# Linear attention on one core: two of pair 3's output stores issued from SyncE in place of GpSimd

## The chip, the core and the metric

The kernel runs on one NeuronCore of a Trainium2 chip. The core has a matrix engine (TensorE, here PE), three engines for elementwise work (VectorE or DVE, ScalarE or ACT, GpSimd or POOL), a SyncE (SP) that here only issues transfers, and 16 DMA engines that move data between the core's memory (SBUF) and HBM. PE writes its results to PSUM, from where DVE or ACT must take them.

A transfer is issued by an engine's instruction and then runs by itself. Those issued by POOL go over a software queue (q0 in the profile, "software_dynamic"), those issued by SP over a hardware queue (q1, "hardware_dynamic"). Both are worked off by the same 16 DMA engines.

The metric is the device time of one execution in microseconds (us), shorter is better. The time before is 125.52 us, the median of three runs (125.43 to 125.59).

## What is computed

Linear attention with the feature map relu(x) + 1, for 8 x 12 heads of 512 rows and 64 columns, float32 in and out:

```python
Q_feat = np.maximum(0, Q) + 1
K_feat = np.maximum(0, K) + 1
KV = np.einsum('bhkd,bhkv->bhdv', K_feat, V)
K_sum = np.sum(K_feat, axis=2)
numerator = np.einsum('bhqd,bhdv->bhqv', Q_feat, KV)
denominator = np.einsum('bhqd,bhd->bhq', Q_feat, K_sum)
return numerator / (denominator[:, :, :, None] + 1e-10)
```

The three inputs are 12.58 MB each and so is the output: 37.75 MB are read from HBM and 12.58 MB written.

## The kernel before

The 96 heads are cut into six equal parts of 16 heads, called pairs and numbered 0 to 5 (each is a pair of halves `n` for keys and values). For one pair, each of Q, K and V is 2 MiB of float32 in HBM; POOL's loads turn it into bfloat16 on the way, so that 1 MiB is written to SBUF. One output pair is 2 MiB of float32 and leaves in two stores of 1 MiB; only the last pair leaves in three (1 MiB, 0.5 MiB, 0.5 MiB), as `stores_of` (line 311) says.

For each pair: `k_features` (line 155, DVE) makes the key features `kf`; `v_block` (168, DVE or ACT) spreads V into a block form `v_all` with a column of ones, which gives the denominators; `keys_values` (183, PE) multiplies the two into PSUM in four parts for each half; `weights` (196, ACT) copies the result to SBUF; `q_features` (172, DVE), `transposes` (205, PE) and `transposed` (212, ACT) bring the query features into the form that PE needs; `out_matmuls` (217, PE) makes one of eight output parts in PSUM; `norms` (231, DVE) takes a reciprocal of the denominators (line 236), multiplies (line 237) and so writes that part into the pair's output tile `o_sb`; `store` (147) sends parts of it to HBM.

The order on each engine is written out by hand in `ORDER` (line 23). A word is a letter for the task, a pair, and indices: `n41` is the norm of pair 4, part 1; `s30` and `s31` are the two stores of pair 3, parts 0 to 3 and parts 4 to 7; `lk5` is the load of pair 5's keys. Each engine works through its own list in order; where a task needs the result of another engine it waits on a semaphore, and everything behind it on that engine waits too. `needs` (270) lists what a task must come after.

What matters around the change:

- POOL's list has all loads first and then ten stores, in the order `s01 s00 s30 s11 s10 s20 s21 s31 s40 s41`. A store waits on POOL until DVE has written its parts: s30 for n30 to n33 (of which n32 comes last in DVE's list), s31 for n34 to n37 (n36 comes last).
- SP's list has `s50 s51 s52`, the last pair's stores. SP also issues the very first load (`load_first_k`, line 124).
- `store` gets the engine that issues it as an argument (line 341), and asks for a single packet only on POOL's queue (line 152). In HBM a row piece of one store is 2 KB long (8 rows of 64 float32).
- The output tiles come from a pool of four buffers (`OUT_BUFS`, line 15). The first key load borrows one, pairs 0 to 3 have one each, and pair 4 takes over that of pair 0, pair 5 that of pair 1. So the first norm of pair 4 (n41) must come after the stores s00 and s01 have landed, and the first norm of pair 5 (n50) after s10 and s11.
- PSUM has two buffers for output parts (`psum`), so PE's `out_matmuls` of a part waits until DVE's norm two parts earlier is through.
- DVE's list around pair 4's begin is `n35 n34 n37 v502 n36 f50 v501 n41 v513 v510 n40 v511 n43 f51 n42 n45 n44 n46 n47 n50 ...`: the key features (f51) and value blocks of pair 5 stand behind n41.

Of the kernel before, what the change touches and what calls it, by code (L numbers as in the profile page):

```python
# [41 lines left out]
        e31 v412 c41 v411 c42 c43 e40 v500 c50 v503 e41 c51 v512 c52 c53 e50 e51  # L42
    """,
    POOL="""
        lv2 lk2 lq2 lv3 lq3 lk3 lv4 lq4 lk4 lq5 lv5 lk5 s01 s00 s30 s11 s10 s20 s21 s31 s40 s41
    """,
    SP="""
        s50 s51 s52
    """,
)  # L50

# [2 lines left out]
def kernel(  # L54
# [12 lines left out]
    nc = tc.nc  # L67
# [66 lines left out]
    def load(x, s, ns=(0, 1)):  # L134
        if x == "q":
            load_q(s)
            return
        if (x, s) not in tiles:
            tiles[x, s] = pools[x].tile([P, 2, ROWS, D], BF16, name=f"{x}_raw")
        t = tiles[x, s]  # L140
        nc.gpsimd.dma_start(  # L141
            out=t[:, ns[0] : ns[-1] + 1], in_=drams[x][:, 2 * s + ns[0] : 2 * s + ns[-1] + 1]
        )
        for n in ns:
            raw[x, s, n] = t[:, n]

    def store(s, parts, engine):
        lo, hi = parts[0], parts[-1] + 1
        engine.dma_start(  # L149
            out=o_dram[:, 8 * s + lo : 8 * s + hi],  # L150
            in_=outs[s][:, lo:hi],
            single_packet=engine is nc.gpsimd,
        )

    def k_features(s, n):
        kf = kf_pool.tile([P, ROWS, 2, D], BF16, name="kf")
        for a in range(2):
            nc.vector.tensor_scalar(  # L158
                out=kf[:, :, a],
                in0=raw["k", s, n],  # L160
                scalar1=shift[:, a : a + 1],
                scalar2=least[:, a : a + 1],
                op0=ALU.add,
                op1=ALU.max,
            )
        kfs[s, n] = kf

    def v_block(s, n, b, copy):
        ps = slice(32 * b, 32 * b + 32)
        copy(out=v_alls[n][ps, :, b * D1 : b * D1 + D], in_=raw["v", s, n][ps])  # L170

    def q_features(s):
        qf = qf_pool.tile([P, R, C, D], BF16, name="qf")
        rows = raw["q", s].rearrange("p (r c) d -> p r c d", r=R)
        for i in range(C // 2):
            cs = slice(2 * i, 2 * i + 2)
            nc.vector.tensor_scalar(  # L177
                out=qf[:, :, cs], in0=rows[:, :, cs],
                scalar1=1.0, scalar2=1.0, op0=ALU.add, op1=ALU.max,
            )  # L180
        qfs[s] = qf

    def keys_values(s, n, part):

        if part == 0:
            kva_pss[s, n] = psum_kva.tile([P, 4 * D1], FP32, name="kva_ps")
        for c in range(part * ROWS // 4, part * ROWS // 4 + ROWS // 4):
            nc.tensor.matmul(  # L188
                kva_pss[s, n],
                lhsT=kfs[s, n][:, c].rearrange("p a d -> p (a d)"),  # L190
                rhs=v_alls[n][:, c],
                start=(c == 0),
                stop=(c == ROWS - 1),
            )

    def weights(s, n):
        kva_ps = kva_pss.pop((s, n))
        for x in range(2):
            for a in range(2):
                nc.scalar.copy(  # L200
                    out=kvas[s % 2][64 * x : 64 * x + 64, 8 * n + a : 8 * n + 8 : 2, x],
                    in_=kva_ps[64 * a : 64 * a + 64].rearrange("p (b d) -> p b d", b=4),
                )

    def transposes(s, i):
        qt_ps = qt_pss[s, i] = psum_qt.tile([P, R, P], BF16, name="qt_ps")
        for r in range(R):
            nc.tensor.transpose(  # L208
                qt_ps[:, r], qfs[s][:, r, 2 * i : 2 * i + 2].rearrange("p x d -> p (x d)"), identity
            )  # L210

    def transposed(s, i, copy):
        if s not in qts:
            qts[s] = mid_pool.tile([P, C // 2, P, R], BF16, name="qt")
        copy(out=qts[s][:, i], in_=qt_pss.pop((s, i)).rearrange("p r q -> p q r"))  # L215

    def out_matmuls(s, part):

        o_ps = o_pss[s, part] = psum.tile([P, 2, BANK], FP32, name="o_ps")
        for c in range(C // 2):  # L220
            for t in range(2):
                h = 2 * part + t
                nc.tensor.matmul(  # L223
                    o_ps[64 * t : 64 * t + 64, c // 2, (c % 2) * W : (c % 2) * W + W],
                    lhsT=qts[s][:, c, 8 * h : 8 * h + 8],
                    rhs=kvas[s % 2][:, h],
                    start=True,
                    stop=True,
                )

    def norms(s, part):
        if s not in outs:
            outs[s] = out_pool.tile([P, 8, C, D], FP32, name="o_sb")
        cells = o_pss.pop((s, part))[:, :, 0 : 2 * W].rearrange("p b (r x) -> p b r x", x=D1)
        recip = recip_pool.tile([P, 2, 4, 1], FP32, name="recip")
        nc.vector.reciprocal(out=recip, in_=cells[:, :, :, D:D1])  # L236
        nc.vector.tensor_tensor(  # L237
            out=outs[s][:, part].rearrange("p (b r) d -> p b r d", b=2),
            in0=cells[:, :, :, 0:D],
            in1=recip.to_broadcast([P, 2, 4, D]),  # L240
            op=ALU.mult,
        )
# [24 lines left out]
    last = NPAIR - 1  # L267
# [43 lines left out]
    def stores_of(s):  # L311

        if s < 0:
            return ()
        return (range(4), range(4, 8)) if s < last else (range(4), range(4, 6), range(6, 8))

    def trace(engine, task):
        x, s, *at = task
        if x == "load":
            load(at[0], s)  # L320
        elif x == "kf":
            k_features(s, at[0])
        elif x == "vb":
            copy = nc.vector.tensor_copy if engine == "DVE" else nc.scalar.copy
            v_block(s, at[0], at[1], copy)
        elif x == "qf":
            q_features(s)
        elif x == "kv":
            keys_values(s, *at)
        elif x == "ev":  # L330
            weights(s, at[0])
        elif x == "tr":
            transposes(s, at[0])
        elif x == "tc":
            transposed(s, at[0], nc.vector.tensor_copy if engine == "DVE" else nc.scalar.copy)
        elif x == "om":
            out_matmuls(s, at[0])
        elif x == "no":
            norms(s, at[0])
        elif x == "st":  # L340
            store(s, stores_of(s)[at[0]], nc.sync if s == last else nc.gpsimd)

    def read(word):
        if word[0] == "l":
# [3 lines left out]
    def trace_all(orders):  # L348

        left = {engine: list(tasks) for engine, tasks in orders.items()}  # L350
        while any(left.values()):
            before = len(done)
            for engine, tasks in left.items():
                while tasks and all(t in done or t[1] < 0 for t in needs(engine, tasks[0])):
                    trace(engine, tasks[0])
                    done.add(tasks.pop(0))
            assert len(done) > before, {e: t[:1] for e, t in left.items()}
# [54 lines left out]
```

## Time and profile before

| | |
|---|---|
| median of three runs | 125.52 us |
| the profiled execution | 125.7 us, span 123.9 us |
| PE busy (share of span) | 79.9 us (64%) |
| DVE | 94.9 us (77%) |
| ACT | 87.1 us (70%) |
| POOL | 25.6 us (21%) |
| HBM read and written | 37.75 and 12.58 MB, 406 GB/s over the span |
| software queue q0 | 6736 packets, 28.84 MB |
| hardware queue q1 | 1216 packets, 3.15 MB |
| granted PE clock, mean | 0.942 |

The span reaches from the first to the last instruction in the trace; the execution's own time has some 1.8 us more around it. Busy times are those in which an engine ran an instruction; waiting and issuing a transfer do not count for PE, DVE, ACT and SP. The bytes of the queues are those written, so a load that turns float32 into bfloat16 counts with half of what it reads from HBM. "Landing" is the moment at which a transfer's semaphore tells that all its data has arrived.

The ten stores on POOL's queue take 0.75 us each to issue, the three on SP's queue 0.37 us each.

### The profile page before, as it was taken

The page shows a single profiled execution, that of the slowest core. Times are in us where ns is not written, and L with a number is a line of the kernel's source. Part 1 is how long each engine was busy: PE and PEld are TensorE (multiplying, and loading weights), DVE is VectorE, ACT ScalarE, POOL GpSimd, SP SyncE. Part 2 cuts the span into 40 slices and gives each one's busy share as a digit, 9 for nine tenths or more (in the row PEclk, how much of TensorE's full clock was granted, in tenths as well). Part 3 has the DMA queues.
Part 4 walks back from the last instruction along what each step waited for, and adds up shares of the span by engine and source line. Part 5 has one row for each costly group of instructions (what it writes and reads, how often), then busy time and mean ns, then how long its engine had stood idle before and what let it go on. Part 6 is the DMA issues. An engine that isn't in the chain of part 4 may idle for free.

```text
span 123.9 us, 2350 instructions
## 1 busy us (share of the span) xinstructions
PE 79.9 (64%) x960; PEld 61.1 (49%) x960; DVE 94.9 (77%) x185; ACT 87.1 (70%) x97; POOL 25.6 (21%) x52
## 2 busy tenths in 40 slices
PE   0000059995696879972599999499897885975000
PEld 0000037883584656851467788268666563753000
DVE  4998996408996996973986996999999299899400
ACT  7548740599999996999509999899999995031000
POOL 6993002400004300060100019000662000220000
PEclk9999999999999999999559999999999999999755
DMA  3999999999999999999999999999999999999992
GB/s 95 333 214 220 220 201 221 213 227 214 200 216 212 227 213 210 222 220 200 212 221 227 205 212 221 213 214 212 216 328 422 414 419 413 417 411 417 408 399 98
DMA packets 7963, 32.13 MB, mean 259 GB/s; under 512 B 528, under 2 KB 528, under 8 KB 7056
## 3 DMA queue, kind: packets, MB, share of 16 engines
q0 software_dynamic: 6736, 28.84, 93.6%
q1 hardware_dynamic: 1216, 3.15, 6.7%
q8 instruction: 7, 0.11, 0.3%
q14 instruction: 4, 0.03, 0.1%
HBM read 37.75 MB, written 12.58 MB: 406 GB/s over the span
## 4 chain that ended last, share of the span: by engine, by line
DMA 32%; DVE 28%; issue 18%; PE 12%; POOL 2%; ACT 2%; DVEq 0%; POOLq 0%
DMA out_dram<-o_sb 18%; DMA q_raw<-in_Q_dram 15%; PE kva_ps L188 9%; DVE o_sb L237 8%; DVE v_all L170 5%; DVE v_all L262 4%; DVE v_all L260 4%; DVE kf L158 3%; DVE recip L236 2%; ACT qt L215 2%; PE o_ps L223 2%; POOL v_raw L141 1%; DVE qf L177 1%; PE qt_ps L208 1%; POOL out_dram L149 1%
## 5 line engine op out<-in xcount | busy, mean ns | idle before, releaser
L188 PE MATMUL kva_ps<-v_all,kf 128*128 128x260 bf16 x384 | 51.9, 287 | 21.6 <-DVE v_all L170 17.7
L188 PEld LDWEIGHTS <-kf 128*128 128x128 bf16 x384 | 36.8, 101 | 30.5 <-DVE v_all L170 19.0
L170 ACT COPY v_all<-v_raw 32x2048 bf16<-32x2048 bf16 x22 | 42.3, 1925 | 4.7 <-DMA v_raw<-in_V_dram 4.2
L237 DVE TENSOR_TENSOR o_sb<-o_ps,recip 128x512 f32<-128x512 f32 x48 | 33.2, 691 | 4.0 <-DMA out_dram<-o_sb 2.4
L215 ACT COPY qt<-qt_ps 128x1024 bf16<-128x1024 bf16 x24 | 23.3, 1016 | 8.1 <-PE qt_ps L208 7.4
L223 PE MATMUL o_ps<-kva,qt 128*64 128x130 bf16 x384 | 19.8, 228 | 12.3 <-DVE o_sb L237 10.2
L200 ACT CAST kva<-kva_ps 64x260 bf16<-64x260 f32 x48 | 18.0, 374 | 11.5 <-PE kva_ps L188 10.9
L223 PEld LDWEIGHTS <-qt 128*64 128x64 bf16 x384 | 12.8, 111 | 20.3 <-DVE o_sb L237 9.8
L170 DVE COPY v_all<-v_raw 32x2048 bf16<-32x2048 bf16 x26 | 17.7, 685 | 5.0 <-DMA v_raw<-in_V_dram 4.5
L158 DVE TENSOR_SCALAR kf<-k_raw,shift,least 128x2048 bf16<-128x2048 bf16 x22 | 17.1, 817 | 3.7 <-DMA k_raw<-in_K_dram 3.6
L141 POOL DMA_DIRECT2D v_raw<-in_V_dram x7 | 5.3, 755 | 52.6 <-ACT v_all L170 29.5
L208 PE MATMUL qt_ps<-identity,qf 128*128 128x128 bf16 x192 | 14.2, 221 | 1.1 <-ACT qt L215 0.8
L208 PEld LDWEIGHTS <-qf 128*128 128x128 bf16 x192 | 11.8, 99 | 2.7 <-issue 0.9
L149 POOL DMA_DIRECT2D out_dram<-o_sb x10 | 7.6, 762 | 26.8 <-DVE recip L236 14.1
L177 DVE TENSOR_SCALAR qf<-q_raw 128x1024 bf16<-128x1024 bf16 x24 | 8.6, 418 | 3.9 <-DMA q_raw<-in_Q_dram 3.9
L236 DVE RECIPROCAL recip<-o_ps 128x8 f32<-128x8 f32 x48 | 9.6, 200 | 2.1 <-PE o_ps L223 1.8
L260 DVE MEMSET v_all<- 128x2600 f32 x2 | 4.5, 2225 | 1.1 <-issue 1.1
L262 DVE COPY v_all<-ones 128x128 bf16<-128x128 bf16 x2 | 5.0, 2492 | 0.2
L132 POOL DMA_DIRECT2D q_raw<-in_Q_dram x6 | 3.9, 646 | 4.6 <-DVE recip L236 4.6
L245 DVE TENSOR_SCALAR odd<-lane 128x1 int32<-128x1 int32 x1 | 4.4, 4377 | 0.0
L141 POOL DMA_DIRECT2D k_raw<-in_K_dram x6 | 4.2, 697 | 0.0
L375 POOL MEMSET kva<- 128x260 bf16 x16 | 4.2, 314 | 0.0
(17 smaller groups left out, 8.9 us busy)
## 6 DMA issues: line engine op xcount, KB each, us to landing
out_dram<-o_sb POOLq DMA_DIRECT2D x10, 1024.0 KB, 16.8
q_raw<-in_Q_dram POOLq DMA_DIRECT2D x6, 1024.0 KB, 20.7
k_raw<-in_K_dram POOLq DMA_DIRECT2D x5, 1024.0 KB, 21.4
v_raw<-in_V_dram POOLq DMA_DIRECT2D x5, 1024.0 KB, 14.7
o_sb<-in_K_dram SPq DMA_DIRECT2D x1, 1024.0 KB, 4.8
v_raw<-in_V_dram POOLq DMA_DIRECT2D x2, 512.0 KB, 8.5
out_dram<-o_sb SPq DMA_DIRECT2D x1, 1024.0 KB, 7.8
out_dram<-o_sb SPq DMA_DIRECT2D x2, 512.0 KB, 7.2
```

What stands on the lines that cost most here:

```text
L141: nc.gpsimd.dma_start(out=t[:, ns[0] : ns[-1] + 1], in_=drams[x][:, 2 * s + ns[0] : 2 * s + ns[-1] + 1])
L158: nc.vector.tensor_scalar(out=kf[:, :, a], in0=raw["k", s, n], scalar1=shift[:, a : a + 1], scalar2=least[:, a : a + 1], op0=ALU.add, op1= ...
L170: copy(out=v_alls[n][ps, :, b * D1 : b * D1 + D], in_=raw["v", s, n][ps])
L177: nc.vector.tensor_scalar(out=qf[:, :, cs], in0=rows[:, :, cs], scalar1=1.0, scalar2=1.0, op0=ALU.add, op1=ALU.max,)
L188: nc.tensor.matmul(kva_pss[s, n], lhsT=kfs[s, n][:, c].rearrange("p a d -> p (a d)"), rhs=v_alls[n][:, c], start=(c == 0), stop=(c == ROWS ...
L200: nc.scalar.copy(out=kvas[s % 2][64 * x : 64 * x + 64, 8 * n + a : 8 * n + 8 : 2, x], in_=kva_ps[64 * a : 64 * a + 64].rearrange("p (b d) ...
L208: nc.tensor.transpose(qt_ps[:, r], qfs[s][:, r, 2 * i : 2 * i + 2].rearrange("p x d -> p (x d)"), identity)
L215: copy(out=qts[s][:, i], in_=qt_pss.pop((s, i)).rearrange("p r q -> p q r"))
L223: nc.tensor.matmul(o_ps[64 * t : 64 * t + 64, c // 2, (c % 2) * W : (c % 2) * W + W], lhsT=qts[s][:, c, 8 * h : 8 * h + 8], rhs=kvas[s % 2 ...
L236: nc.vector.reciprocal(out=recip, in_=cells[:, :, :, D:D1])
L237: nc.vector.tensor_tensor(out=outs[s][:, part].rearrange("p (b r) d -> p b r d", b=2), in0=cells[:, :, :, 0:D], in1=recip.to_broadcast([P, ...
L262: nc.vector.tensor_copy(out=v_alls[i].rearrange("p c (b d) -> p c b d", b=4)[:, :, :, D], in_=ones[:, None, :].to_broadcast([P, ROWS, 4]),)
```

## The change

The stores s30 and s31 are taken out of POOL's list and put at the head of SP's list. `trace` now lets a store go over SP's queue if it stands in SP's list, where it asked for the last pair before; for s50, s51 and s52 that is the same. With this, `store` asks for no single packet for s30 and s31. Nothing else differs, and all other lists are as they were.

```diff
     POOL="""
-        lv2 lk2 lq2 lv3 lq3 lk3 lv4 lq4 lk4 lq5 lv5 lk5 s01 s00 s30 s11 s10 s20 s21 s31 s40 s41
+        lv2 lk2 lq2 lv3 lq3 lk3 lv4 lq4 lk4 lq5 lv5 lk5 s01 s00 s11 s10 s20 s21 s40 s41
     """,
     SP="""
-        s50 s51 s52
+        s30 s31 s50 s51 s52
     """,
...
         elif x == "st":
-            store(s, stores_of(s)[at[0]], nc.sync if s == last else nc.gpsimd)
+            store(s, stores_of(s)[at[0]], nc.sync if engine == "SP" else nc.gpsimd)
```

## The prediction

> **What bounds the kernel now.** I read the page's 40 slices first, then the chain of waits, then the order of DMA issues on POOL and SP, and last the DMA queues in short stretches around the place that changes.
>
> ```profile
> DMA  3999999999999999999999999999999999999992
> GB/s 95 333 214 220 220 201 221 213 227 214 200 216 212 227 213 210 222 220 200 212 221 227 205 212 221 213 214 212 216 328 422 414 419 413 417 411 417 408 399 98
> ```
>
> The 16 DMA engines are full from about 2 us to 121 us. Loads (float32 read, bf16 written) show some 214 GB/s of written bytes until 91 us; the stores run at some 415 GB/s after that. No engine is near that: DVE has 77%. So the span is the DMA work plus what lies before and behind it, and an edit can lengthen it in two ways: more DMA time per byte, or a stretch in which the engines have nothing queued.
>
> ```profile
> 76.48 21.70 DMA out_dram<-o_sb
> 98.17 0.03 issue
> ```
> ```profile
> 98.29 0.69 DVE L237 TENSOR_TENSOR o_sb<-o_ps,recip 128x512 f32<-128x512 f32 x1 [2.42 <-DMA out_dram<-o_sb]
> ```
>
> The chain shows the one place where a store holds up compute. The second software-queue store (s00) is issued at 76.48 and lands at 98.17. DVE's n41, the first norm of pair 4, writes into pair 0's output buffer, so it waits 2.42 us for that landing. From there to 116.01 DVE is busy almost without a gap (0.34 and 0.18 us of waits for PE).
>
> ```profile
> 75.70 1.54 POOL L149 DMA_DIRECT2D out_dram<-o_sb  x2
> 87.94 3.77 POOL L149 DMA_DIRECT2D out_dram<-o_sb  x5 [10.70 <-DVE o_sb L237]
> 93.67 0.75 POOL L149 DMA_DIRECT2D out_dram<-o_sb  x1 [1.96 <-DVE o_sb L237]
> 105.52 0.75 POOL L149 DMA_DIRECT2D out_dram<-o_sb  x1 [11.10 <-DVE recip L236]
> 109.31 0.75 POOL L149 DMA_DIRECT2D out_dram<-o_sb  x1 [3.04 <-DVE recip L236]
> ```
> ```profile
> 112.68 3.73 SPq L149 DMA_DIRECT2D out_dram<-o_sb  x3
> ```
>
> In the written order these are s01 s00, then s30 s11 s10 s20 s21 (held until n32 has written pair 3's first half at 87.64), s31, s40, s41; on SP s50, s51, s52. Landing is issue plus the time to landing: s01 94.8, s00 98.2, s30 100.4, s31 113.0, s40 115.4, s41 118.6, s50 120.5, s52 123.0. Work is queued 5 to 20 us deep.
>
> **The change, step by step.** Nothing is computed differently.
>
> *Bytes and packets.* s30 and s31 (1 MiB each) leave the software queue for SP's hardware queue. Both kinds can be priced from stretches where one queue ran alone, 100 to 112 us and 118.3 to 120.3 us:
>
> ```profile
> q0 software_dynamic: 1292, 4.97, 102.0%
> ```
> ```profile
> q1 hardware_dynamic: 420, 0.82, 105.3%
> ```
>
> The software queue moves 4 KB a packet, the hardware queue 2 KB. By the mean rates of these stretches (415 and 409 GB/s) 1.049 MB takes 2.53 and 2.56 us, 0.03 us more; by bytes per busy share (4.97 MB in 12.24 us, 0.82 MB in 2.106 us, that is 406 and 389 GB/s) it takes 2.58 and 2.70, 0.11 us more. Two stores: +0.06 to +0.22 us. I take +0.13, near the middle, and it counts in full since DMA is full.
>
> *POOL.* It loses two issues (2 x 0.75 us) and, above all, its wait for n32: s11, s10 and s20 are ready at once, so they are issued behind s00 from 77.2, and s21 after n26 at 82.3 in place of 91. They only queue up earlier behind loads that last until 91 to 92 us; nobody waits for them before n50 at 109. If the queue's room ran out, POOL would wait with nothing behind it until s40 at 105.5. Worth 0.
>
> *SP.* Two issues of 0.37 us at about 87.7 (n32) and 93.4 (n36), both before anything that moves. Behind them on SP stand only s50 to s52, 19 us later. Worth 0 as issues.
>
> *Sharing.* s30 and s31 no longer stand in line behind s01 and s00; they compete with them. What s00 loses, n41 waits longer. The trace has one comparable overlap: s50, issued at 112.68 while s40 and s41 were queued. The queues from 113.1 to 115.2, 115.3 to 116.3 and 116.3 to 117.3:
>
> ```profile
> q0 software_dynamic: 223, 0.86, 101.2%
> ```
> ```profile
> q0 software_dynamic: 86, 0.32, 79.4%
> q1 hardware_dynamic: 45, 0.09, 23.6%
> ```
> ```profile
> q1 hardware_dynamic: 149, 0.31, 78.2%
> q0 software_dynamic: 32, 0.10, 24.4%
> ```
>
> The hardware queue got nothing until 115.3, 2.6 us after its issue; SP's load at the start, with the engines empty, was issued at 0.74 and moved its first bytes at 1.73, after 1.0 us. Then it came in by packets, mostly as engines ran out of s41; s41 landed 3.2 us behind s40 instead of the usual 2.5, so it lost some 0.7 us. If packets of 2 KB and 4 KB alternate one for one, a software store loses half of 2.57 us, 1.3 us, when it is shared from end to end.
>
> For s30: issued 87.7, its packets come in at 90 or so, the loads end at 91 to 92, and what is already lined up covers about the first us of s01. The remaining 4 us of s01 and s00 are shared and lose half their time: d = 2.0 us. Bounds: 0, if the hardware queue is served only when the other is dry (the first of the three stretches); 5.1, if both stores (2 x 2.57) go through whole before s00. I take 2.0, the value nearest to what s41 showed.
>
> The Trainium skill (DMA: Bandwidth & Descriptors, "Queues, rings and completion order") says that each DMA engine takes the queues it has work for in turn, a packet at a time. By that rule with no late start, from 88.7 on, each of some 10 remaining load packets and 32 store packets per engine would let one 2 KB packet of 0.08 us (2.57 us over 32) in, so d would be 3.4 us, an estimate from that page; the stretch at 113 us, where nothing was let in, differs.
>
> *What d does.* DVE reaches n41 at 95.87 as before and waits until about 100.2 instead of 98.2. Everything after shifts by D = 2.0: s40 to 107.5, s41 to 111.3, s50 to 114.7, s52 to 118.0. Is the DMA still fed? Loads end at about 91.5, and the nine stores s0 to s3 and s40 are 9 x 2.53 us of work, so they last until about 114.3 on the mean and 115 on the last engine (s40 landed at 115.4), in either kernel. s41 has 3.7 us to get there. s41 then covers until about 117.7, and s50, issued 112.7 + D, must deliver by then: with 2.6 us from issue to first packet that needs D below 2.4, with 1.0 us D below 4.0. s52 (1.3 us long) has more room. So at D = 2.0 the longer stall is hidden by queued stores, with 0.4 to 2.0 us to spare. If that cover is gone, each us of D above it costs one.
>
> Sum: +0.13 us. The profiled execution took 125.7 us (span 123.9 and 1.8 around it), 0.2 over the median 125.52; I carry the difference to the median: **125.65 us**, +0.1%.
>
> **Rivals.**
>
> *The stall grows past its cover (slower).* Its place is PE while n41 waits. PE frees PSUM through DVE's norms, and today it stands still only 0.48 us there; with d = 2.0 it stands still for 2.5 us. In this trace the clock was halved after a thin stretch:
>
> ```profile
> 54.96:58.38 3.42, 1.42 (x24) 0.96 (x22) 0.66 (x3) 3.40 (x2) 0.03 (x1) 1.00 1.02 210
> 58.38:61.79 3.41, 1.58 (x13) 1.14 (x14) 3.31 (x10) 2.31 (x2) 0.56 (x1) 0.50 1.06 213
> ...
> 102.75:106.16 3.41, 2.14 (x28) 1.54 (x29) 3.34 (x8) 1.49 (x4) 0.64 (x1) 1.00 1.04 422
> ```
>
> Columns: stretch and its length, PE busy, PEld, DVE, ACT, POOL, granted clock, DMA share, GB/s. PE busy 1.42 of 3.42 us was followed by clock 0.50; 2.14 was not (nor 2.02, the least since PE got going). With 2.0 us more idle, the stretch from 99.34 falls from 2.98 to about 1.6, between the two. At half clock eight L188 matmuls took 1.91 us instead of 1.07. The next two stretches hold 2.14 + 3.12 = 5.26 us of PE work; times 1.75 that is 9.2 in 6.8 us, at most 2.4 us late, about 1.3 after PE's later gaps. D is then 3.3, up to 4.4: against a cover of 2.4 to 4.0 the loss is 0 to 2.0, typically 0.6, so **126.2 us**. The other way into this rival is d = 5.1: s50 at 117.8, plus 1.0 to 2.6, plus 5.1 for the three last stores, is 123 to 125.5 where the data now ends at 122.7: up to 127.9. It decides from D above 2.4 to 4.0. Against it: at 115 us the hardware queue came in late and thinly. The Trainium skill (TensorE: Matmul & The Clock Gate, "The HAM clock gate") has the gate judged in free-running windows of about 3.4 us, so by it the drop could come in some executions (126.2) and not in others (125.65); the two stretches above agree with that length.
>
> *The change does not do what it says (no change).* The hardware stores wait until the software queue is dry, about 107. Then d = 0, n41 waits 2.4 as now, and only the packet cost stays: 125.6 us.
>
> *A more even finish (faster).* From 120.3 to 122.7 the hardware queue has 52% of the engines: some end over 1 us before the last. If mixing the queues levelled half of that, about 0.55 us is gained: **125.0 us**. Nothing in the trace says that it would; the bytes per engine are the same.
>
> **How the numbers follow.** Forecast 0.50 (its own range 125.4 to 125.85), stall past its cover 0.32, no sharing 0.10, more even finish 0.08. About 0.2% (0.25 us) is what a measurement of this kernel can tell from no change. Slower: 0.29 of the rival and 0.12 of the forecast's upper edge, 0.41. Faster: 0.08 and 0.04, 0.12. Same: 0.47. The range, 125.3 to 126.7, leaves out about 0.1 below and 0.08 above.
>
> **What would show it.** Right: s30 on SP at about 87.7 and s31 at 93.4; four stores on POOL between 77 and 83; n41's wait for the DMA at 4 to 5 us; s52 issued near 118; DMA slices still 9 to the end; the last store's data ending 0.1 to 0.2 us later. Wrong: n41's wait still 2.4 (no sharing) or over 5 (whole stores ahead); PEclk at 0.50 after 102 us; a DMA slice under 9 between 112 and 120, which would mean that the cover was too short.

## The result and the profile after

The changed kernel takes 125.67 us (median of 13 runs, 125.28 to 125.88) where the kernel before takes 125.40 us in the same session (13 runs, 125.22 to 125.59). The ratio is 1.0021 with a 95% interval of 1.0012 to 1.0029: 0.27 us slower, between 0.15 and 0.36. A second measurement in another session gave 1.0015 (1.0003 to 1.0027). So it is a small loss, about 0.15 to 0.2%, of the sign that was forecast, and larger than the forecast's 0.13 us.

There are two profiles of the changed kernel, one from each session. They differ in how far DVE had come when the stall began, so both are shown. First, the page's slices and the issues on POOL and SP in the first one:

```profile
DMA  3999999999999999999999999999999999999993
GB/s 90 336 212 216 215 212 215 216 232 220 192 214 212 231 215 199 223 218 208 212 214 228 211 208 226 220 202 212 212 313 419 411 417 410 421 411 415 408 409 152
```
```profile
74.92 3.83 POOL L149 DMA_DIRECT2D out_dram<-o_sb  x5
82.89 0.75 POOL L149 DMA_DIRECT2D out_dram<-o_sb  x1 [4.14 <-DVE o_sb L237]
106.45 0.75 POOL L149 DMA_DIRECT2D out_dram<-o_sb  x1 [22.81 <-DVE recip L236]
110.24 0.75 POOL L149 DMA_DIRECT2D out_dram<-o_sb  x1 [3.04 <-DVE recip L236]
```

The DMA engines are as full as before, from start to end. On POOL, s11, s10 and s20 now go out directly behind s01 and s00 (74.92 to 78.75), and s21 at 82.89; s40 and s41 follow 0.93 us later than before. On SP, s30 goes out at 89.26.

The wait of n41 in DVE's timeline, in the first and in the second profile of the changed kernel:

```profile
99.23 0.69 DVE L237 TENSOR_TENSOR o_sb<-o_ps,recip 128x512 f32<-128x512 f32 x1 [1.96 <-DMA out_dram<-o_sb]
```
```profile
95.77 0.21 DVE L236 RECIPROCAL recip<-o_ps 128x8 f32<-128x8 f32 x1
100.42 0.69 DVE L237 TENSOR_TENSOR o_sb<-o_ps,recip 128x512 f32<-128x512 f32 x1 [4.44 <-DMA out_dram<-o_sb]
```

Before, n41 ran at 98.29 after 2.42 us of waiting. In the second profile DVE arrives as early as before (95.98) and then waits 4.44 us, so n41 is D = 2.13 us late. In the first, DVE came 1.4 us later by itself and s30 went out later, so that D is only 0.94. The chain of waits still runs through that store:

```profile
75.69 23.42 DMA out_dram<-o_sb
```

Before, this piece was 21.70 us long, for the same store, issued at 76.48. What made it longer stands in the queues of the second profile, from 91 to 92, 92 to 93 and 93 to 94 us:

```profile
q0 software_dynamic: 76, 0.30, 83.9%
q1 hardware_dynamic: 26, 0.05, 14.4%
```
```profile
q0 software_dynamic: 73, 0.29, 69.9%
q1 hardware_dynamic: 63, 0.13, 33.1%
```
```profile
q0 software_dynamic: 71, 0.26, 65.0%
q1 hardware_dynamic: 75, 0.15, 39.5%
```

Columns: packets, MB, share of the engines' time. s30 was issued at 87.86, and from 88 to 91 the hardware queue had not one packet. Then it came in and settled at one packet of 2 KB for one of 4 KB. The span of these two profiled executions is 123.5 us, 0.4 less than the profile of before, although the medians stand the other way: these two executions took 125.28 and 125.29 us and are among the fastest of theirs, while the profile of before is of a run of 125.7 us, longer than any of the 13 here. A profile of this kernel can therefore show mechanisms and rates, but not the 0.27 us itself.

### The profile page after: what moved, and what is told of

Its sections match the earlier page's. It is cut to its first block, busy times and chain, and to the rows that moved or that the text cites. A ratio compares the mean times of both kernels' runs of the same rounds, so it can differ in the third digit from the quotient of the medians.

```text
span 123.5 us, 2350 instructions
## 1 busy us (share of the span) xinstructions
PE 83.3 (67%) x960; PEld 62.8 (51%) x960; DVE 95.1 (77%) x185; ACT 87.1 (71%) x97; POOL 23.5 (19%) x50
## 4 chain that ended last, share of the span: by engine, by line
DMA 32%; DVE 28%; issue 18%; PE 12%; POOL 3%; ACT 2%; DVEq 0%; POOLq 0%
DMA out_dram<-o_sb 19%; DMA q_raw<-in_Q_dram 13%; PE kva_ps L188 10%; DVE o_sb L237 8%; DVE v_all L170 5%; DVE v_all L262 4%; DVE v_all L260 4%; DVE kf L158 3%; DVE recip L236 2%; ACT qt L215 2%; PE o_ps L223 2%; POOL v_raw L141 1%; DVE qf L177 1%; PE qt_ps L208 1%; POOL out_dram L149 1%
## 5 line engine op out<-in xcount | busy, mean ns | idle before, releaser
L188 PE MATMUL kva_ps<-v_all,kf 128*128 128x260 bf16 x384 | 55.4, 300 | 20.8 <-DVE v_all L170 17.7
L188 PEld LDWEIGHTS <-kf 128*128 128x128 bf16 x384 | 38.5, 106 | 31.7 <-DVE v_all L170 18.6
L149 POOL DMA_DIRECT2D out_dram<-o_sb x8 | 6.1, 766 | 30.0 <-DVE recip L236 25.9
L132 POOL DMA_DIRECT2D q_raw<-in_Q_dram x6 | 3.4, 566 | 4.4 <-DVE recip L236 4.4
```

The source lines that it names most:

```text
L188: nc.tensor.matmul(kva_pss[s, n], lhsT=kfs[s, n][:, c].rearrange("p a d -> p (a d)"), rhs=v_alls[n][:, c], start=(c == 0), stop=(c == ROWS ...
```

## The experiments

Each was timed against the kernel before on the same chip; "us" differences are the ratio less one times the median of before, with the 95% interval.

**Only the order on POOL** (e1_order).

```diff
-  ... lk5 s01 s00 s30 s11 s10 s20 s21 s31 s40 s41
+  ... lk5 s01 s00 s11 s10 s20 s21 s30 s31 s40 s41
```

> All ten stores stay on POOL's software queue; only their order is the changed kernel's (s30 and s31 behind s21). Three theories for the +0.27 us of the change: (A) the 2 KB packets of the hardware queue cost DMA time, 0.03 to 0.11 us a store by the rows of before, 0.13 for each store if they are to explain all of it; (B) n41's longer wait comes through to the end; (C) two queues at work at once cost DMA time by themselves. Here none of the three is in it: all expect 0 +- 0.15 us, n41's wait as before (about 2 us). A loss here would mean that the order on POOL is the cause and that all three are wrong.

Measured: 1.0007 (0.9995 to 1.0019), +0.09 us (-0.06 to +0.24), and n41 waited 2.15 us. The order on POOL and the earlier issue of four stores are not what costs, as far as 0.2 us can be told.

**No single packet for s30 and s31, still on the software queue** (e2_small2).

```diff
-            single_packet=engine is nc.gpsimd,
+            single_packet=engine is nc.gpsimd and s != 3,
```

> The kernel before, in which s30 and s31 alone ask for no single packet on the software queue; order and queues are as before. A: their packets become 2 KB as on the hardware queue (q0 gains 1024 packets of 2 KB in place of 512 of 4 KB) and the time rises by 0.06 to 0.27 us with no longer wait at n41. B and C: 0 +- 0.1 us. If the packets stay at 4 KB the run tells nothing on A.

Measured: 1.0003 (0.9987 to 1.0019). The packets stayed as they were (7963 in all, as before), so this says nothing on packet size. It shows that the request by itself is neither seen in the packets nor in the time.

**s30 and s31 late, behind s40 on SP** (e4_late).

```diff
 POOL: ... lk5 s01 s00 s11 s10 s20 s21 s41
 SP:   s40 s30 s31 s50 s51 s52
```

> s40, s30 and s31 go over SP's queue, in this order, so that s30 and s31 are issued only at about 105 us, after n42, when s00 has long landed. Three stores have 2 KB packets, n41's wait is as before, and the two queues share from 105 us to the end. A: 3/2 of the change's cost, +0.1 to +0.4 us. B: 0 +- 0.1. C: about half of the change's cost or less, +0.1, since the shared stretch is shorter (the changed kernel shares from 93 to 108 us).

Measured: 1.0063 (1.0040 to 1.0086), +0.79 us (0.50 to 1.08), more than any of the three expected. Here is the DMA in this run from 104.5 to 107.5, an us a line (PE, PEld, DVE, ACT, POOL, clock, DMA share, GB/s):

```profile
104.50:105.50 1.00, 1.00 (x10) 0.70 (x10) 0.93 (x4) 0.00 (x0) 0.00 (x0) 1.00 1.02 418
105.50:106.50 1.00, 1.00 (x15) 0.83 (x15) 0.97 (x3) 0.00 (x0) 0.00 (x0) 1.00 0.80 324
106.50:107.50 1.00, 1.00 (x21) 0.67 (x20) 0.66 (x2) 0.00 (x0) 0.00 (x0) 1.00 1.05 383
```

POOL has only six stores to queue before n42, and SP sits in order behind s40; so some engines had nothing from 105.5 on until s40's first packets came. The experiment took away n41's longer wait but added a dry queue (324 and 383 GB/s after 418, some 0.3 us of work), and one engine ended its share of s31 2 us behind the next. Its 0.79 us cannot be split between these, so it does not tell A, B and C apart. The last experiment repeats it without the dry queue.

**s20 and s21 on SP as well** (e5_four).

```diff
 POOL: ... lk5 s01 s00 s11 s10 s40 s41
 SP:   s20 s21 s30 s31 s50 s51 s52
```

> s20 and s21 also go over SP's queue, ahead of s30 and s31; they are ready at about 72 and 82 us, so they share with the last loads and with s01 and s00. At one packet for one packet the loads of pair 5 land up to 5 us later (64 packets of 0.08 us for each engine), and n41 starts some 4 to 6 us later than before. A alone: four stores in 2 KB packets, +0.25 to +0.55 us. With the cover worked out in the prediction (D below 2.4 to 4.0 us) the delay comes through here: +1 to +4 us in all, DMA slices under 9 near the end. B: more than 4 us.

Measured: 1.0056 (1.0039 to 1.0073), +0.70 us (0.49 to 0.92), and n41 at 100.89, 2.6 us later than before and not 4 to 6. Part of that is a flaw of the experiment: with s20 and s21 ahead, the pool gives pair 4 the buffer of pair 2 and not that of pair 0, so n41 waits for s21 here and not for s00 (which landed only at 104.4, after n41 had run). This wait is 1.71 us, shorter than before; the delay comes from the keys of pair 5, for which DVE waited 2.52 us just ahead. Beside loads too the queues take turns one for one, from 80 to 88 us:

```profile
q0 software_dynamic: 291, 1.31, 79.8%
q1 hardware_dynamic: 291, 0.60, 21.8%
```

A 2 KB packet goes in for each 4 KB that a load writes; the last keys were 22.1 us on their way in place of 17.3. The span ended 0.4 us later after the last data than in the other runs (last section), so that some 0.3 us are left for four stores and the delay together. In this run PE worked only 0.60 us between 96.2 and 99.6 us, and then its clock was halved (0.50 in the line; columns as above):

```profile
99.60:103.00 3.40, 3.40 (x27) 1.94 (x26) 2.07 (x4) 2.83 (x2) 0.00 (x0) 0.50 1.03 411
```

**The changed kernel again** (after_again).

> The changed kernel once more, for a second estimate and a second profile beside the next three. All theories: +0.15 to +0.36 us against before, the interval of its first measurement; n41's wait 2 to 4.5 us, packets of s30 and s31 one for one with the software queue's from about 93 to 108 us.

Measured: 125.66 us, 1.0015 (1.0003 to 1.0027), +0.19 us (0.04 to 0.34). Its profile is the second one above.

**A single packet asked for on SP's queue** (e6_hwsingle).

```diff
-            single_packet=engine is nc.gpsimd,
+            single_packet=True,
```

> The changed kernel, in which SP's five stores ask for a single packet as POOL's do. If that makes 4 KB packets on the hardware queue, A expects the cost to go and a little more (all five stores gain): -0.1 to +0.1 us against before; B and C expect the change's +0.27 still. If the packets stay at 2 KB and alternate as in the changed kernel, all expect +0.27; if a whole store becomes one turn of the queue, n41's wait grows to 5 us or more and its cover is tested.

Measured: 1.0016 (1.0004 to 1.0029), +0.20 us. The hardware queue's packets stayed at 2 KB (845 of them for 1.70 MB from 94 to 106 us) and alternated as before. So this is a third measurement of the change rather than a test of A.

**s40 and s41 on SP as well** (e7_hw4).

```diff
 POOL: ... lk5 s01 s00 s11 s10 s20 s21
 SP:   s30 s31 s40 s41 s50 s51 s52
```

> s40 and s41 go over SP's queue as well, so that POOL issues only s01 s00 s11 s10 s20 s21. A: four stores in 2 KB packets, twice the change's cost, +0.25 to +0.55 us. C: the two queues share for the same 15 us as in the changed kernel, so +0.27 as it. B: the same wait at n41 as in the changed kernel, so +0.27.

Measured: 1.0064 (1.0052 to 1.0076), +0.80 us (0.65 to 0.95), above all expectations. The last data landed at 122.64, as in the profile of before (122.67), but 1.7 us passed from there to the span's end instead of 1.2. Without this half us some 0.3 us are left for four stores, within A's range. That subtraction mixes one profile with medians, so I take it as agreeing, not as shown.

**All stores on SP** (e8_all).

```diff
 POOL: ... lk5
 SP:   s30 s01 s00 s11 s10 s20 s21 s31 s40 s41 s50 s51 s52
```

> All stores go over SP's queue, s30 first so that none is issued before about 88 us; the software queue has only loads, and the two share only until the last load ends at about 92. A: ten stores in 2 KB packets: +0.6 us at 0.06 each (the rows of before), +1.3 at the 0.13 each that would explain the whole change. C: almost no shared stretch, 0 to +0.1. B: s00 now stands behind s30 and s01, so n41 waits some 2 to 3 us longer, as much as in the forecast; +0.2 to +0.3 if that comes through.

Measured: 1.0057 (1.0045 to 1.0070), +0.71 us (0.56 to 0.88), 0.07 us for each of ten stores. The queues from 94 to 106 us, in the kernel before, in the changed kernel (second profile) and in this one:

```profile
DMA packets 1295, 5.01 MB, mean 417 GB/s; under 512 B 76, under 2 KB 76, under 8 KB 1293
...
q0 software_dynamic: 1293, 4.99, 101.9%
```
```profile
DMA packets 1687, 4.96 MB, mean 413 GB/s; under 512 B 66, under 2 KB 66, under 8 KB 1686
...
q0 software_dynamic: 844, 3.25, 66.3%
q1 hardware_dynamic: 842, 1.69, 36.4%
```
```profile
DMA packets 2451, 4.89 MB, mean 407 GB/s; under 512 B 71, under 2 KB 71, under 8 KB 2450
...
q1 hardware_dynamic: 2450, 4.87, 104.8%
```

With 4 KB packets alone it is 417 GB/s, with the two in turn 413, with 2 KB packets alone 407. Other profiles narrow what the first two numbers can say: in the same window e1_order, with 4 KB packets alone, has 415, and the two in turn have 414 in the first profile of the change and 416 in e6_hwsingle. So 413 to 416 in turn cannot be told from 415 to 417; only the 407 stands apart, and it comes from one queue alone, not from mixing. From 417 to 407 is 2.4%, 0.06 us for a store of 2.5 us, and ten of them make 0.6 of the measured 0.71. n41 waited 4.44 us here too, so B's part, if any, is in this run as well; the DMA share stays at 1.05 from 111 to 119 us, which shows no empty stretch. This speaks for A at the size that the rows of before gave, and against C. Some of the 0.71 may lie behind the data: the profiled execution of this kernel has 2.0 us around its span where the others have 1.8, and 0.1 us more between its last data and the span's end. Taken off, 0.04 us a store is left.

**All stores on POOL** (e9_pool).

```diff
-        ... s31 s40 s41
+        ... s31 s40 s41 s50 s51 s52
-            store(s, stores_of(s)[at[0]], nc.sync if s == last else nc.gpsimd)
+            store(s, stores_of(s)[at[0]], nc.gpsimd)
```

> The change the other way round: s50, s51 and s52 too go over POOL's software queue, so that all 12.58 MB leave in 4 KB packets. A: two MiB less in 2 KB packets, -0.13 us, against which stands the later start of the last stores (0.75 us to issue for 0.37 and a slower way to the first packet), which the queue covers as long as it holds work: -0.2 to +0.3 us. If the 2 KB packets cost nothing, 0 to +0.4.

Measured: 1.0094 (1.0080 to 1.0108), +1.18 us, far outside. The DMA engines from 117 to 125 us, 0.2 us a digit:

```profile
DMA  9899999989998998998676531100000000000000
```

The data ended at 122.3, before the 122.67 of the kernel before. That is no proof of a gain from 4 KB packets, since both profiles of the changed kernel, with more 2 KB packets, end at 122.25. The span went on to 124.8: 2.5 us of nothing, where 1.2 is usual, and these 1.3 us are more than the whole loss. In the trace SP was through at 122.93, and POOL's part of the closing steps, in which all engines wait for one another, came only at 124.13. So this run says little on packets.

**A longer wait without a second queue** (e10_wait).

```diff
-  ... lk5 s01 s00 s30 s11 s10 s20 s21 s31 s40 s41
+  ... lk5 s30 s01 s00 s11 s10 s20 s21 s31 s40 s41
```

> The kernel before with s30 put ahead of s01 and s00 on POOL; all on the software queue, 4 KB packets. POOL waits for n32 (87.6 us) before it issues s01 and s00, the loads last until 91 to 92, so s00 lands one store (2.5 us) later, n41 waits about 4.9 us in place of 2.4 and all behind it is 2.5 us late. B: the longer wait alone brings at least the change's +0.2 us. The forecast's cover (D up to 2.4 to 4.0 us is hidden by queued stores): 0 +- 0.15.

Measured: 1.0024 (1.0014 to 1.0035), +0.30 us (0.18 to 0.44), n41 at 100.89 after 4.85 us, D = 2.6. That is B's figure and not the zero expected from the forecast's cover at this D. From 111 to 119 us, in the kernel before, the changed kernel (second profile, D = 2.1) and this one:

```profile
111.00:119.00 8.00, 1.96 (x38) 1.12 (x32) 4.81 (x12) 1.03 (x3) 0.00 (x0) 0.84 1.03 410
```
```profile
111.00:119.00 8.00, 3.90 (x64) 2.58 (x64) 6.68 (x17) 1.50 (x4) 0.75 (x1) 0.87 1.02 407
```
```profile
111.00:119.00 8.00, 4.49 (x73) 2.93 (x72) 7.14 (x17) 1.50 (x4) 0.75 (x1) 0.86 1.00 399
```

The last two numbers are DMA share and GB/s. At D = 2.6 the DMA runs 2.7% below that of before for 8 us: 0.2 us of small gaps while the last stores are late. At D = 2.1 it is 0.7%, 0.06 us, hardly more than profiles without a longer wait differ (410 before, 412 in e1_order). So at 2.6 the queued work no longer hides the delay in full, and at 2.1 no loss can be told.

**A wait of two stores** (e11_wait2).

```diff
-  ... lk5 s01 s00 s30 s11 s10 s20 s21 s31 s40 s41
+  ... lk5 s30 s11 s01 s00 s10 s20 s21 s31 s40 s41
```

> The same with s30 and s11 ahead of s01 and s00: n41 is 5.0 us late, s50 is issued at about 117.7 where s41 ends at 117.7. Past the cover of 2.4 to 4.0 us: +1.0 to +2.6 us, with DMA slices under 9 between 112 and 120. If the cover is wider than worked out: under +0.5.

Measured: 1.0114 (1.0087 to 1.0140), +1.43 us (1.09 to 1.76), as expected; n41 waited 7.18 us and came 4.9 late. Two stretches of this run:

```profile
104.00:106.00 2.00, 2.00 (x19) 1.66 (x20) 1.95 (x4) 0.38 (x1) 0.00 (x0) 0.50 1.01 414
...
114.00:116.00 2.00, 1.71 (x28) 1.23 (x26) 1.85 (x5) 0.24 (x1) 0.75 (x1) 1.00 0.29 115
```

The columns after the length are PE, PEld, DVE, ACT, POOL, clock, DMA share and GB/s. PE stood still for 5.26 us while n41 waited; after that the clock is 0.50 until some 109 us, which neither the changed kernel nor e10_wait shows there (e5_four does, from 99.6 to 103.0). From 114 to 116 the DMA has a share of 0.29, a hole of 1.4 us.

**Two stores on SP without the longer wait** (e12_two_late).

```diff
 POOL: ... lk5 s01 s00 s11 s10 s20 s21 s30 s41
 SP:   s40 s31 s50 s51 s52
```

> Two stores on SP's queue as in the change, but s40 and s31, in this order, issued at about 105 us when n42 is through; POOL keeps s01 s00 s11 s10 s20 s21 s30 s41, so that its queue lasts until about 108.6 and does not run dry. n41's wait is that of the kernel before (about 2 us), and nothing behind it moves. What is left of the change is two stores in 2 KB packets beside the software queue. If the packets (A) make all of the change's cost, +0.15 to +0.35 us; if they cost what the rows say, +0.06 to +0.15, and the rest of the change is its longer wait (B), as in the kernel with s30 ahead of s01; if neither, 0.

Measured: 1.0017 (1.0002 to 1.0031), +0.21 us (0.03 to 0.39), with n41 waiting only 1.49 us and running 1.0 us earlier than before. Two stores on SP's queue and no longer wait cost as much as the change. So the change's loss needs no contribution from the wait, though the interval leaves room for one. The two queues share here as well, so this run does not tell A from C; that rests on e8_all.

## Why the prediction was right, step by step

*What bounds the kernel.* Right for the change: the engines stay full in both kernels. In the experiments the losses came as bytes that take longer, as an empty queue, or, in e5_four, e7_hw4, e8_all and e9_pool, in part behind the last data.

*Bytes and packets, +0.13 us.* Right in kind, probably a little small. The per-store price from the rows of before was 0.03 to 0.11 us, 0.065 taken. Measured with ten stores it is 0.04 to 0.07, which makes 0.08 to 0.14 for two. The changed kernel measured 0.27 and 0.19 us, and 0.20 in the variant that asks for single packets; only the first interval (0.15 to 0.36) excludes 0.14, by a hair.

*POOL and SP, nothing.* Right: the issues went as forecast, and the order alone measured 0.09 (-0.06 to +0.24).

*Sharing, d = 2.0 us.* Right: n41 came 2.13 us late where DVE arrived as before, and 0.94 us where DVE was itself late. The way there was right too: a late first packet (nothing for 3 us after s30's issue), then one for one (844 and 842 packets in 12 us). So the rule of the Trainium skill (DMA: Bandwidth & Descriptors, "Queues, rings and completion order") that the engines take the queues in turn by packets agrees with this trace. Its unit here is one packet of 2 or 4 KB, so the hardware queue gets half of the other's bytes. What the rule alone would have missed is the late start, with which the prediction came to 2.0 instead of the 3.4 of the rule without it; measured were 2.1.

*The cover, D below 2.4 to 4.0.* About right, with a softer edge. At 2.1 no loss of DMA rate can be told, at 2.6 about 0.2 us is gone, and at 4.9 (e11_wait2, where s50 was issued 5.2 us later than before) the whole kernel lost 1.4. If each us above the cover costs one, the last of these puts its end at 3.5 to 3.8 us, inside the range; but small losses begin at 2.6 already, near the lower bound, which came from the 2.6 us between the issue and the first packet of s50. The forecast was thus closer to the edge than its "0.4 to 2.0 us to spare" says.

*The sum.* Right in sign, and half the measured size. That 125.65 was forecast and 125.67 measured is in part luck, since the kernel before took 125.40 us beside it and not 125.52. The rates from 94 to 119 us, in the kernel before, in the changed kernel (second profile) and with all stores on SP (e8_all):

```profile
94.00:119.00 25.00, 15.64 (x208) 11.00 (x206) 18.38 (x40) 11.41 (x18) 1.93 (x3) 0.95 1.03 414
```
```profile
94.00:119.00 25.00, 15.86 (x210) 11.19 (x207) 18.48 (x40) 11.71 (x18) 1.51 (x2) 0.96 1.03 413
```
```profile
94.00:119.00 25.00, 15.65 (x208) 11.01 (x206) 18.29 (x40) 11.52 (x18) 0.00 (x0) 0.96 1.05 407
```

The last number is GB/s. From 414 to 413 is some 0.06 us, from 414 to 407 some 0.4 us. The first profile of the change has 413 too, e6_hwsingle 414, e12_two_late 412 and e1_order 414. So of the change's 0.19 to 0.27 us the profiles show some 0.1 us at most as lower rate, about what the forecast counted; the rest stays open. The two profiled executions of the change ran at 125.3 us, while most of its runs stand at 125.5 to 125.9.

*The last data.* Not as forecast in the profiles of the change: they show it at 122.25, 0.4 us earlier than before and not 0.1 to 0.2 later. Yet at 119 us a little more was left to move (1.07 and 1.05 MB, before 1.02), so it is the end that was more even. In e6_hwsingle, whose order and packets are those of the change, the data ended at 122.73, 0.06 us later than before. The end thus differs between executions by more than the change costs; why is open.

*The rivals.* The stall past its cover is a real mechanism, shown by e10_wait and e11_wait2, but in the profiles the change stops just short of it. Its first way, the halved clock, did not follow n41's wait in the changed kernel at D of 2.1, where PE stood still for 2.40 us, nor in e10_wait at 2.6. It did in e5_four at 2.6, where DVE had waited for keys as well, and at 4.9, after 5.26 us in which PE stood still. "No sharing" was wrong by the packet counts. A more even finish was seen in both profiles of the change and not in e6_hwsingle; the medians show no gain from it.

## What to carry to other kernels

Where all DMA engines were full, a second queue moved no more bytes (413 GB/s against 414); look at what packets it makes (2 KB instead of 4 KB cost 2.4% of the rate in e8_all) and at whom it delays. Here the transfers on the second queue took turns with everything queued on the first, so the first task that waited for the first queue got 2 us later. Whether that costs is read at the end: compare the delay with how long the queued work lasts until the delayed transfers are needed.

## What was not expected of the hardware

Asking for a single packet, or not asking, changed no packet size on either queue (7963 packets with and without on the software queue for s30 and s31; 2 KB on the hardware queue with and without).

The time from the last data to the span's end is 1.2 to 1.3 us in most kernels here. With the last store on POOL's queue (e9_pool) it was 2.5 us, with POOL's closing step 1.2 us behind SP's. In the two kernels in which POOL issued six stores (e5_four, e7_hw4) it was 1.7; with seven, eight, ten or none it was 1.2 to 1.4. In these two the extra time is one pause: POOL stands still for 0.42 us between two of its closing steps, where every other trace has 0.07 or less. The same two traces have an 8 KB transfer on the instruction queue q14 at the span's very end (from 124.39 us in e7_hw4 and 124.46 in e5_four). In e8_all, whose time around the span is 0.2 us longer, such a transfer runs after the span's end (125.73); the other traces have their last one at 122 us or before. That these transfers and the lost time belong together is suggested by this and not shown, and why they fall there is open.
